# Hybrid decoder trunk on one core: block inverse by 32x32 and 64x64 products, scale sums on VectorE, key products by quarters, gates in row groups, accumulating DMAs

## The chip, the core and the metric

The kernel runs on one core of a Trainium2 chip. The metric is device time in microseconds, one launch, one core. PE is TensorE (matrix products into PSUM, weight loads beside them), DVE is VectorE, ACT is ScalarE, POOL is GpSimd, SP is the engine whose queue starts the DMAs.

## What is computed

One layer on a sequence of 1024 tokens of width 1024, all in float32. The parts that the change touches:

```python
mod = c_act @ w_mod[l] + b_mod[l]
sh1, sc1, g1, sh2, sc2, g2 = jnp.split(mod[:, None, :], N_MOD, axis=-1)
h = rms_norm(x, norm_mix_w[l]) * (1.0 + sc1) + sh1
proj = h @ w_in[l]
...
r_pre = jnp.einsum('bsgi,gij->bsgj', xb, lru_gate_a_w[l]) ...   # 8 blocks of 64x64
i_pre = jnp.einsum('bsgi,gij->bsgj', xb, lru_gate_x_w[l]) ...
...
decay = jnp.exp(jnp.where(causal, g[..., :, None] - g[..., None, :], -jnp.inf))
Lmat = jnp.where(strict, jnp.einsum('bhnid,bhnjd->bhnij', k_beta, k) * decay, 0.0)
tmat = Lmat + jnp.eye(C, dtype=jnp.float32)
u = lax.linalg.triangular_solve(tmat, v_beta, ...)
w = lax.linalg.triangular_solve(tmat, k_beta * jnp.exp(g)[..., None], ...)
...
mix = jnp.concatenate([out_lru, out_gdn], axis=-1) @ w_out[l]
x = x + g1 * mix
x = x + g2 * (jnp.square(jax.nn.relu(h @ w_up[l])) @ w_down[l])
```

## The kernel before

**Stages.** Tokens are normalised and transposed into `hT` (eight blocks of 128 channels, each as a rounded high part and a low remainder). Then 24 projections of 128 columns each run over all tokens: four keys k, four z, four pairs q and v, four pairs lx and ly. Keys feed the gated delta rule with chunks of 128 tokens (32 chunks: 4 heads by 8), lx and ly feed the RG-LRU. The output projection (`wg` for the delta rule's half, `wl` for the LRU's half), the second norm, and the MLP by a scheme of seven products (`upx`, `upy`, `upz`, then `dn`) follow and are not touched by the change, apart from their order.

**Precision.** The large products take three float32r products each (high by high, high by low, low by high: `mm3`, L575). Small ones are plain float32, which the trace shows as two PE instructions per product.

**Order.** Nothing is issued where it is written. `Recorder.add` (L220) records every operation; `schedule` (L267) simulates the engines with cost constants and writes one order per engine; `emit` plays it. Products marked `bb` (the large ones) give way to any small product that is ready. `SHIFTS`, a packed table, moves single operations by priority. So a change to any cost constant or to `SHIFTS` can reorder all queues.

**Start.** The SP queue loads x tiles 0 to 3, the eight tiles of the scale `sc1` (4 MB in runs of 512 columns), the key weights k0 and k1, `wab`, x tiles 4 to 7, then eight tiles for `sh1` (L676 to L691). `sc1` is a vector-matrix product done in two halves (L795 to L814): five of eight rows are summed on ACT and DVE (`macc`), three more and the sum are added by PE products with one output row (`sc_r`), copied to a row and turned into a column by PE (`sc_c`). Only when both halves are there are all `hT` blocks scaled, and the thirds of k0 and k1 (342 tokens each, `third`) can run. The key loop ends with k2 and k3 in line with the other projections (L1223).

**Weights.** `Proj.split` (L731) rounds a weight tile on ACT (`_wh`) and subtracts it on POOL or DVE (`_wl`).

**Decay and the block inverse.** `decay` (L912) loads the broadcast gate sums, adds the mask on POOL and takes eight ACT exponentials; it runs for each key and once more for each query. `key` (L933) multiplies the decay by `bcoef` (beta over the key's squared norm), multiplies it into k k^T and leaves the result in `LT`; `inverse` (L968) then

- solves the 32x32 diagonal blocks by 31 DVE steps of two instructions (`gg`, `xx`, `ftmp`),
- spreads them into 128x128 block-diagonal matrices `xn`, `xt`, with POOL clearing,
- and combines by four rounds of 32 products of 128x128 float32: `ie`, `ig`, `ih`, `ix`.

`chain` (L1097) then walks the eight chunks of a head with `LT`.

**LRU.** `lru` (L1182) convolves lx, splits the result on ACT and POOL (for the last block on DVE: `xrl`), and multiplies it by the gate weights, padded from two 64x64 blocks to 128x128 (`gwt`, `gwh`, `gwl`): for each of four channel blocks, two gates and two token halves three products of 512 tokens, 48 in all. `msum` gathers the squares on POOL.

Of the kernel before, what the change touches and what calls it, by code (L numbers as in the profile page):

```python
# [22 lines left out]
P = 128  # L23
# [24 lines left out]
SC1_SUM = 5  # L48
# [3 lines left out]
LOAD_WINDOW, DUE = 40.0, 5.0  # L52
RESERVE = {"b": 11, "ps": 2, "u": 1, "c": 2}


class Buf:


    def __init__(self, pool, tag, bufs, shape, dt, name, proto):
        self.pool, self.tag, self.bufs, self.shape, self.dt, self.name, self.proto = pool, tag, bufs, shape, dt, name, proto  # L60
        self.tile = None
        self.key = (id(pool), tag)
        self.left = 0
        self.last = 0.0
        self.held = False
        self.pri = 1e9
        self.sum = None
# [53 lines left out]
def dram_box(ap):  # L121
# [7 lines left out]
    'c-qaId2m(NeaC<AJ?ZI5LLdnV0RkZwiG4R<wm^)7YrMprIwncm)J@}Qn;B2s&a}-;-8P+MlCeAWA6YtW)=nmlGmY(z3C0fC21AT77@NiHn8ip4f%'  # L129
    'X-NC;j^Qo%_IG`(AS%vFr1jyS#hvx%Zsk`7Phy@0^#`w7v|jSNWjw&9C+Kw%f@gO~HjJheRg#*x5f{vi-x<OUf<RRC=f{IG#@j$BiBGF_eaG+uxu'  # L130
    '0_O5~3b>G0Eo_FtW8hH2o?GNZ}bLLu6`uV|I2Oq!m-usK({d=@J9o>#ro%nn2TN|U~Tjz`hBr-xS>2PV$J)AF+Cp1UWdXn=AvOzcNo4S+p<+4r>>'
    'JBZW=2VGGLP|vScKMQ|ptuytP<iOeyG!JI@<94#*(2j*TY9S``wv_^qcQ2=dxP4?`w|%*$N08LF27ZW(gu-Q$&nr{<=Z<{KGCHgZWuq-$QNZmUx5'
    'c>>3N9^anz>?dL=SODr7p8lqK>xxHO<m@}~UTd)}p2`uZeWySBrDv~H1IaQ?JTme0sy$<Mtd_p$h9_+xZJFKLHX@XadOEL-Gv@`ko(z0Tr`9eT-|'
    'cSor4XrfN5V>!~K)ux~NliYl%=KJkh<oeWsZ1n3{MzJ2cpc_*!Cvs%Cl*&jcW-Qmnb|)su&GhEH7Sr$JT1k&9C11u%4Zn@XaMq|J<Q<*HHk!@1rI'
    'qxwRR`$%zc&6%zI0(jU4DJlz}4eY%rke$47n94Kcq*IxM?z5=DE=+N5X_(CdKW%C8#q<or&xR>8b6FVw^Q;5{<2+$31YjO;78AETpnL_o#QR@!nt'
    'Q)^42{uZG8QYWHg#&CHcv#_S&Sdba$D%;H|I6lC<R2dj~$P9@S*A#;$?2iT8fw5s6Wbe^tdtmZIc(>b%+2{_uVWpWCB_Aqvpa#-hiw{s#gwNlE@`'
    'qgUDb)G!@Pd%r3GFzwWEBcRm99#CfdqV@VYvbFFlrN`mWyo$L<D7&?v(dEAprc8+P|B8%jKtWRv=zx*s9$@L{B68*DEt++el@v@!|4u3J=f47-Ks'
    'C>(>lt1B`8DC+NA8%X7r#6%A*~(@V$x93N-yLEX5l66fG-*!#i)#4i>Pj&TMPg9*|!k5#Qnb5p2>^Tz`V?VaDX!+?^w%XwfKISS|DE^DLPxeR|nS'
    'T~8Tw{Z6A>X?i#SHF8ZeT4nNM?;nX}DCM1bP?1M(hC9lpd<}XU64{Pjt&=v+_R3G>Tk<co=iBl_`0)s5tB`_G@1t>!mNP!99NmuePj)mP9<7zn%A'
    'K;1^F`2DSs?duoQn^gBa>u3GUQ*1y=(MlfdX#IQmS4;vOgX_o5xoFv3#rB`zwLO$E3@<rs=(JX;=RmlR;Sh;DJhxLmbXftXmw*lFvRLlu?ddk2!z'  # L140
# [67 lines left out]
class Recorder:  # L208
# [58 lines left out]
    def schedule(self):  # L267
# [36 lines left out]
        while done < len(ops):  # L304
# [34 lines left out]
            for b in op.allocs:  # L339
# [15 lines left out]
                elif f[0][0] > t + 1e-6:  # L355
                    wait = ("t", f[0][0])
# [1323 lines left out]
```

## Time and profile before

| | |
|---|---|
| median of 3 runs | 1164.93 us (1164.21 to 1165.41) |
| span of the profiled execution | 1162.6 us |
| busy: PE, DVE, ACT, POOL | 1137.1, 834.6, 616.5, 371.4 us |
| mean DMA rate | 197 GB/s |
| mean granted PE clock | 0.997 |

The span runs from the first to the last instruction of the one profiled execution; the runs' times also hold what lies around it, 2.3 us by the median. A group's busy time counts time in which at least one of its matrix products was in the pipe; to price one product the distance between the starts of neighbours is the better measure, and the prediction uses that.

### The profile page before, as it was taken

Reading aid. Unit: us, or ns where it says so; the run is one execution under the profiler, and the core shown is the slowest. Engines: PE = TensorE matmul, PEld = TensorE weight load, DVE = VectorE, ACT = ScalarE, POOL = GpSimd, SP = SyncE. Lnnn points to the kernel's source line nnn. Section 1 sums busy time; section 2 is a strip of 40 time slices with the busy share of each in tenths; the row PEclk is TensorE's granted clock in tenths of the full one; section 3 lists DMA queues with packets and bytes.
Section 4 is the critical chain, followed back from the end, with each engine's and each line's share of the span. In section 5 each row is a group of like instructions: output and inputs, shape, how many; then the busy total and the mean of one; then the engine's idle time right before and its main releaser. Section 6 shows DMA issues by size and latency. Waiting matters only on the chain.

```text
span 1162.6 us, 15986 instructions
## 1 busy us (share of the span) xinstructions
PE 1137.1 (98%) x5952; PEld 979.8 (84%) x5952; DVE 834.6 (72%) x1123; ACT 616.5 (53%) x988; POOL 371.4 (32%) x221
## 2 busy tenths in 40 slices
PE   6899999999999999999999999999999999999997
PEld 3799999999999998887888888887888888888885
DVE  5778786687986879778776776766885583865563
ACT  5547445445547866477655555556644533363441
POOL 1329512253424463300003231311450057723030
PEclk9999999999999999999999999999999999999999
DMA  9623432544454462422276887773999956864541
GB/s 338 223 86 110 134 121 75 180 121 159 152 185 145 135 230 107 145 84 80 65 267 237 274 281 247 252 244 136 364 403 388 369 175 247 308 226 168 199 163 72
DMA packets 127151, 229.52 MB, mean 197 GB/s; under 512 B 10657, under 2 KB 51806, under 8 KB 127074
## 3 DMA queue, kind: packets, MB, share of 16 engines
q1 hardware_dynamic: 127074, 228.51, 56.7%
q8 instruction: 46, 0.75, 0.3%
q14 instruction: 31, 0.25, 0.1%
HBM read 171.83 MB, written 56.65 MB: 197 GB/s over the span
## 4 chain that ended last, share of the span: by engine, by line
PE 91%; DMA 3%; DVE 3%; ACT 1%; issue 1%; SPq 1%; POOL 0%; POOLq 0%; ACTq 0%
PE dn L427 26%; PE upx L427 15%; PE upz L427 8%; PE wg L427 4%; PE upy L427 4%; PE wl L427 4%; PE z_p L427 4%; PE lx_p L427 4%; PE q_p L427 4%; PE ly_p L427 4%; PE v_p L427 3%; PE k_p L427 2%; PE ch L427 2%; SPq L427 1%; DMA sh_w<-in_w_mod_dram 1%
## 5 line engine op out<-in xcount | busy, mean ns | idle before, releaser
L427 PE MATMUL upx<-h2h,U 128*128 128x512 f32 x512 | 168.0, 394 | 0.0
L427 POOL TENSOR_TENSOR wd<-wd,wd 128x512 f32<-128x512 f32 x32 | 49.9, 1568 | 214.4 <-DMA wd<-in_w_down_dram 163.4
L427 PEld LDWEIGHTS upx<-h2h,U 128*128 128x128 f32 x512 | 96.0, 188 | 22.5
L427 PE MATMUL upx<-h2l,U 128*128 128x512 f32 x256 | 100.8, 394 | 0.0
L427 DVE TENSOR_TENSOR U<-wu,U 128x512 fp32r<-128x512 f32 x112 | 85.0, 774 | 18.1 <-ACT U L427 17.9
L427 ACT ACTIVATE act<-act 128x512 f32<-128x512 f32 x112 | 70.3, 632 | 44.9 <-DVE act L427 43.2
L427 PE MATMUL upz<-h2h,U 128*128 128x512 f32 x256 | 85.0, 394 | 0.0
L427 ACT CAST U<-wu 128x512 fp32r<-128x512 f32 x112 | 66.8, 617 | 27.8 <-DVE wu L427 10.0
L427 PEld LDWEIGHTS upx<-h2l,U 128*128 128x128 f32 x256 | 48.1, 188 | 11.5
L427 PEld LDWEIGHTS upz<-h2h,U 128*128 128x128 f32 x256 | 48.1, 188 | 11.4
L427 DVE TENSOR_TENSOR act<-upz,ek 128x512 f32<-128x512 f32 x32 | 22.1, 690 | 40.1 <-PE upz L427 25.9
L427 ACT COPY ek<-upx 128x512 f32<-128x512 f32 x48 | 28.0, 584 | 42.6 <-PE upx L427 42.4
L427 PE MATMUL upz<-h2l,U 128*128 128x512 f32 x128 | 50.4, 394 | 0.0
L427 POOL TENSOR_TENSOR R<-R,R_5o 128x1024 f32<-128x1024 f32 x8 | 20.0, 2520 | 74.4 <-DMA R<-in_w_down_dram 63.2
L427 PE MATMUL upy<-h2h,U 128*128 128x512 f32 x128 | 42.7, 394 | 0.0
L427 POOL TENSOR_TENSOR ssq<-ssq,mhalf 128x1 f32<-128x1 f32 x16 | 11.6, 725 | 84.8 <-DVE ssq L427 84.8
L427 DVE TENSOR_TENSOR wu<-wu,wu 128x512 f32<-128x512 f32 x48 | 36.1, 759 | 0.5 <-DMA wu<-in_w_up_dram 0.4
L427 ACT ACTIVATE vn<-ch,bcoef 128x128 f32<-128x128 f32 x32 | 11.8, 368 | 45.0 <-PE ch L427 44.9
L427 PE MATMUL k_p<-hh,k_wh 128*128 128x342 f32 x96 | 31.9, 332 | 1.0 <-ACT hh L427 1.0
L427 PE MATMUL k_p<-hl,k_wh 128*128 128x342 f32 x96 | 32.0, 333 | 0.8 <-DVE hl L427 0.8
L427 PE MATMUL k_p<-hh,k_wl 128*128 128x342 f32 x96 | 31.9, 332 | 0.0
L427 PE MATMUL ly_p<-hh,ly_wh 128*128 128x342 f32 x96 | 31.7, 330 | 0.0
(574 smaller groups left out, 3719.3 us busy)
## 6 DMA issues: line engine op xcount, KB each, us to landing
L<-aod SPq DMA_DIRECT2D x56, 512.0 KB, 6.5
R<-in_w_down_dram SPq DMA_DIRECT2D x40, 512.0 KB, 5.9
wu<-in_w_up_dram SPq DMA_DIRECT2D x32, 512.0 KB, 5.0
aod<-as SPq DMA_DIRECT2D x64, 256.0 KB, 3.3
wd<-in_w_down_dram SPq DMA_DIRECT2D x32, 512.0 KB, 6.5
aod<-act SPq DMA_DIRECT2D x48, 256.0 KB, 2.9
x<-in_x_dram SPq DMA_DIRECT2D x16, 512.0 KB, 4.6
sc_w<-in_w_mod_dram SPq DMA_DIRECT2D x16, 512.0 KB, 7.2
```

The source lines that it names most:

```text
L427: op.fn(*[res(v) for v in op.a], **{n: res(v) for n, v in op.k.items()})
```

## The change

The diff does the following.

- **Scale sums.** `sc1` comes in four quarters of 256 columns; all eight rows of a quarter are summed on ACT (one) and DVE (seven); PE only turns the sum into a column.
- **Keys by quarters.** The weights of all four keys come as four tiles of two channel blocks each (`wk0` to `wk3`). A class `Key` multiplies, for tokens 0 to 511, each pair of channel blocks as soon as its quarter of `sc1` is known, then tokens 512 to 767 (`second(0)`) and 768 to 1025 (`second(1)`). The first pair runs in two halves of 256 tokens. DMA order at the start is rewritten for this; 36 products of constants (`warm`) are recorded at a lowest priority `FILL`.
- **Weights.** `Proj.split` writes minus the high part with ACT and lets a DMA from the POOL queue add the raw weight to it. The same is done for the LRU's low part; `msum` and the decay mask are also added by such DMAs.
- **Decay** is made once per head, stored to DRAM and loaded again by the query. `bcoef` leaves it and goes to the small blocks of the inverse, the key's gate factor goes from a POOL product to a factor in `chain`.
- **Inverse.** Blocks of 32 are joined to 64 by five 32x32 products per chunk (`level1`), blocks of 64 to 128 by two 64x64 products per chunk (`level2`).
- **Gates.** The two 64x64 blocks stay apart: each product contracts over 64 rows and gives both gates, in pairs on the two halves of the rows.
- **Order.** Planner constants (SP issue, DMA lanes, start) and `SHIFTS` are new.

```diff
+FILL, WARM, AB_DUR, GATE_DUR, L1A_DUR, L1B_DUR, L2_DUR = 1e6, 36, 0.85, 0.89, 0.12, 0.2, 0.14
...
+class Adder(Proxy):
...
+            self.rec.add("POOL", fn, (), {"out": out, "in_": in_, "accum_op": ALU.add}, [out], [in_, out], ADD_ISSUE)
...
+    GD = Adder(rec, "POOL", nc.gpsimd)
...
+    load_x(0)
+    load_sc1(0)
...
+    load_x(1)
+    load_wk(0)
+    load_x(2, 3)
+    for q in range(1, 4):
+        load_sc1(q)
+        load_wk(q)
+    load_x(4, 5, 6, 7)
...
             A.copy(self.w[0], raw)
-            e.tensor_tensor(out=self.w[1], in0=raw, in1=self.w[0].bitcast(F32), op=ALU.subtract)
+            A.mul(self.w[1], self.w[0].bitcast(F32), -1.0)
+            GD.dma_start(out=self.w[1].bitcast(F32), in_=raw)
...
+    def scale1(q):
+        acc = big(f"sc1_acc{q}")[:, 0:256]
+        for k in range(NK):
+            macc(acc, sc1_w[q, k // 4][:, k % 4, :], k)
+        pc = ps(f"sc1_c{q}")
+        for j in range(2):
+            mm(pc[:, j:j + 1], acc[:, j * P:(j + 1) * P], ones[:, 0:1])
...
+    for q in range(1, 4):
+        scale1(q)
+        splitk(q, V if q == 1 else G)
+        for k in (2 * q, 2 * q + 1):
             xhalf(0, k)
+        for h in range(NH):
+            projs[h].first(q, 0, 512)
+    warm = ps("warm")
+    for i in range(WARM):
+        mm(warm[:, i % 4 * P:i % 4 * P + P], ident, triu)
+        rec.ops[-1].bias = FILL
...
+    def decay(h):
+        dm = big(f"k{h}_dm")
+        SP.dma_start(out=v3(dm), in_=neg[:, None, :].to_broadcast([P, 8, P]))
+        GD.dma_start(out=dm, in_=gdr[h:h + 1, :].to_broadcast([P, T]))
...
+        def level1(g):
+            gs = slice(16 * g, 16 * g + 16)
+            p = ps(f"it{g}")
+            for q in range(16):
+                i, c = 16 * g + q, slice(32 * q, 32 * q + 32)
+                mms(L1A_DUR, [(p[blk[b + 1], c], LT[blk[b], i, blk[b + 1]], xnc[blk[b], i, :], True, True) for b in (0, 2)], 0.25)
...
+                mms(L1B_DUR, [(p[blk[0], c], tt[blk[1], i, :], xtc[blk[1], i, :], True, True),
+                              (p[blk[2], c], tt[blk[3], i, :], xtc[blk[3], i, :], True, True),
+                              (p[blk[1], c], xtc[blk[1], i, :], tt[blk[1], i, :], True, True)], 0.25)
...
+        def level2(h):
...
+            for q in range(8):
+                mms(L2_DUR, [(p[up, 64 * q:64 * q + 64], LT[lo, 8 * h + q, up], w[lo, q, :], True, True)], 0.5)
+            A.mul(w[up], v3(p, 64)[up], -1.0)
...
+                mms(L2_DUR, [(p[lo, 64 * q:64 * q + 64], w[up, q, :], LT[up, 8 * h + q, up], True, True)], 0.5)
+            V.tensor_copy(LT[lo, hs, up], v3(p, 64)[lo])
...
-        (V if ct == 3 else G).tensor_tensor(out=xl_, in0=xr, in1=xh.bitcast(F32), op=ALU.subtract)
...
+        A.mul(xl_, xh.bitcast(F32), -1.0)
+        GD.dma_start(out=xl_.bitcast(F32), in_=xr)
+        cs = slice(ct * P, (ct + 1) * P)
+        for s in halves:
+            pair = [ps(f"gate{ct}{s.start}{e}") for e in range(2)]
+            mms(GATE_DUR, [(p, w[64 * e:64 * e + 64, cs], x_[64 * e:64 * e + 64, s], i == 0, i == 2)
+                           for i, (w, x_) in enumerate(((gwh, xh), (gwh, xl_), (gwl, xh))) for e, p in enumerate(pair)])
+            for e, p in enumerate(pair):
+                r = slice(64 * e, 64 * e + 64)
+                A.activation(ta[r, s], p[0:64, :], AF.Tanh, scale=0.5, bias=hab[r, ct:ct + 1])
+                A.activation(ti[r, s], p[64:128, :], AF.Tanh, scale=0.5, bias=hxb[r, ct:ct + 1])
```

396 lines of the change are left out of this document (224 added, 172 removed).

## The prediction

> **What bounds the kernel now.** First the page, then busy time by stretches, then PE's waits.
>
> ```profile
> span 1162.6 us, 15986 instructions
> PE 1137.1 (98%) x5952; PEld 979.8 (84%) x5952; DVE 834.6 (72%) x1123; ACT 616.5 (53%) x988; POOL 371.4 (32%) x221
> ```
> ```profile
> 0.00:15.00 15.00, 7.29 (x29) 4.57 (x30) 7.01 (x20) 7.96 (x12) 4.26 (x13) 1.00 0.86 316
> 15.00:30.00 15.00, 12.57 (x54) 5.87 (x52) 9.30 (x25) 9.50 (x16) 1.65 (x3) 1.00 1.07 363
> 30.00:45.00 15.00, 11.46 (x66) 9.17 (x66) 11.41 (x15) 9.35 (x14) 0.55 (x1) 0.93 0.79 286
> 45.00:60.00 15.00, 14.49 (x95) 12.90 (x94) 11.04 (x23) 5.08 (x8) 8.02 (x3) 0.96 0.54 146
> 60.00:1140.00 1080.00, 1076.36 (x5649) 935.41 (x5650) 788.02 (x1028) 578.91 (x928) 354.68 (x197) 1.00 0.56 195
> ```
> ```profile
> PE h2T L427 <- DVE h2r L427: 1.1, 2, 0.6
> PE ktok L427 <- DVE k2T L427: 0.9, 1, 0.9
> ```
>
> The columns of the second fence are the stretch and its length, then busy time of PE, PEld, DVE, ACT and POOL, the granted clock, the DMA share and GB/s. From 60 to 1140 us PE is idle 3.6 us of 1080; its longest wait is 1.1 us in total. So from 60 us on PE products are the bound: a microsecond of PE work removed there is a microsecond of the end, and work moved off POOL is worth nothing by itself. Up to 60 us PE is idle 14.2 us, and at times slowed (clock 0.93 and 0.96). To price PE work I use distances between starts, from the chain of waits, where products stand back to back:
>
> ```profile
> 119.58 33.12 PE z_p L427 x211
> ```
> ```profile
> 843.31 306.12 PE dn L427 x1320
> ```
>
> A three-part product of 342 columns costs 33.12 / 211 = 0.157 us per part, of 512 columns 306.12 / 1320 = 0.232.
>
> **The start.** Here PE's time up to 60 us is divided into work that any version must do and the rest.
>
> ```profile
> L427 PE MATMUL xTp<-ident,x 128*128 128x128 f32 x64 | 12.7, 332 | 1.7 <-ACT x L427 0.8 <-DVE rs L427 0.3 <-DVE x L427 0.2
> L427 PE MATMUL k_p<-hh,k_wh 128*128 128x342 f32 x32 | 11.2, 352 | 1.0 <-ACT hh L427 1.0
> ```
> ```profile
> L427 PE MATMUL k_p<-hh,k_wl 128*128 128x342 f32 x31 | 10.8, 349 | 0.0
> L427 PE MATMUL sc_r<-sc_w,cact 128*1 128x512 f32 x12 | 5.8, 591 | 1.4 <-DMA sc_w<-in_w_mod_dram 1.3
> L427 PE MATMUL ab<-hl,wab 128*16 128x342 f32 x16 | 5.1, 323 | 0.0
> ```
> ```profile
> L427 PE MATMUL sc_c<-ones,sc_row 1*128 1x1 f32 x16 | 2.1, 248 | 0.0
> L427 PE MATMUL sc_r<-sc_acc,ones 128*1 128x512 f32 x4 | 2.0, 592 | 0.0
> L427 PE MATMUL sh_c<-ones,sh_acc 128*128 128x1 f32 x15 | 1.7, 245 | 0.0
> ```
>
> Lasting work: 95 parts of k at 0.157 (14.9; 32, 32 and 31 in three groups), 32 of ab (5.0; two groups of 16), 64 transposes at 0.112 (7.2; that distance is shown below), sh_c 1.7: 29 us. The other 31 us of the 60 are loss: idle, slow clock, 9.9 us of `sc_r` and `sc_c`, pipe ends. How much of it is lost after the change follows from what comes when:
>
> ```profile
> GB/s 0 38 385 391 388 385 404 396 385 392 384 389 381 307 273 234 426 410 421 407 385 410 421 401 410 315 39 6 189 288 149 249 238 120 29 285 46 0 172 178
> ```
> ```profile
> 11.55 3.11 DVE L427 SCALAR_TENSOR_TENSOR sc_acc<-sc_w,cact,sc_acc 128x512 f32<-128x512 f32 x4 [0.70 <-ACT sc_acc L427]
> ```
> ```profile
> 22.01 2.73 DVE L427 SCALAR_TENSOR_TENSOR hl<-xTp,A,hh 128x512 fp32r<-128x512 f32 x4 [0.74 <-ACT hh L427]
> ```
> ```profile
> 34.51 2.60 DVE L427 SCALAR_TENSOR_TENSOR sh_acc<-sh_w,cact,sh_acc 128x1024 f32<-128x1024 f32 x2 [0.89 <-ACT sh_acc L427]
> ```
> ```profile
> 145.79 0.43 DVE L427 TENSOR_TENSOR ftmp<-gg,xx 128x256 f32<-128x256 f32 x1
> ```
>
> The first row has the DMA rate from 0 to 60 us in 40 slices: about 388 GB/s from 2 us on, so a tile of 0.524 MB takes 1.35 us. In the new order x0 and the first scale quarter (three tiles) are there at 1.5 + 4.1 = 5.6 us. DVE then adds seven rows of 256 columns (0.43 each by the last row, as a row of 512 costs 3.11 / 4 = 0.78), 3.0 us, with one scaling of x between (at most the 1.3 of a row of 1024 columns, 2.60 / 2): 9.9 us; column product, two short DVE steps and the first eighth of `hT` end at about 13 us, as I estimate,, where the key products begin. From there PE has 24 parts per quarter at 0.232, for four quarters 22.3 us (twice as many at half the price where 256 columns are taken), and 32 transposes, 3.6: until 38.9 us. Behind it the DMA needs 1.5 + 16 x 1.35 = 23.1 us for all sixteen tiles, DVE 12.0 for scale sums (28 x 0.43 instead of 8 x 0.78 = 6.2), 5.8 for `hl` (six of 2.73 / 4 = 0.68 and four of 0.43), at most 7.8 for six steps of 1024 columns on x and the weights, 25.6 us in all, starting at 6: both ahead of PE. Next come x4 to x7 (28.5 us), and `second(0)` with the two first thirds of ab, 96 at 0.116 and 32 at 0.157, 16.1 us of PE. That covers the sums for `sh1` (tiles at 39 us, seven DVE rows of 1.3 us, 9.1 us), on which only `second(1)` waits; were they late, PE would be idle by that much. Loss then: 13 us before the first product, `sc_c` 1.8 (16 instructions of 1.7 / 15, like sh_c), and 4 us that I put for seams between these four sequences: 19 instead of 31, **gain 12**. Ends: 16 (no seams), and -2, if the 5.8 us more DVE work stands in the way and the 36 `warm` products (72 instructions at 0.112, 8.1 us) stand in PE's queue ahead of ready work instead of in gaps.
>
> **The inverse.** Before: the four groups `ie`, `ig`, `ih`, `ix`, 32 products and 64 instructions each.
>
> ```profile
> 167.70 0.40 PE L427 MATMUL v_p<-hh,v_wl 128*128 128x342 f32 x1
> 167.94 0.32 PE L427 MATMUL v_p<-hh,v_wh 128*128 128x342 f32 x1
> ```
> ```profile
> 169.76 5.30 PE L427 MATMUL ie<-xn,LT 128*128 128x128 f32 x46
> 174.90 4.41 PE L427 MATMUL ig<-xt,ee 128*128 128x128 f32 x38
> ```
> ```profile
> L427 PEld LDWEIGHTS upy<-h2h,U 128*128 128x128 f32 x128 | 24.0, 188 | 5.6
> ```
> ```profile
> L427 PEld LDWEIGHTS ab<-hl,wab 128*16 128x16 f32 x24 | 2.3, 95 | 1.5 <-DVE hl L427 0.2
> ```
>
> From 169.76 to 174.90 stand 46 instructions: 0.112 each, so 256 cost **28.6 us**. After: 160 products of 32x32 and 64 of 64x64, 320 and 128 instructions. No row has both few weights and few columns. A weight load of 16 columns takes 95 ns, of 128 columns 188: 0.83 ns per column, so loads shrink with the block. If the whole distance shrinks so, with 5 ns fixed, it is 0.033 for 32 and 0.059 for 64: 10.6 + 7.6 = 18.2, with 16 changes of shape at 0.08 (1.3; the first of two parts of v after `ie` takes 0.24 to the next start and not 0.157) 19.5: **gain 9.1**. I take this one, as it is nearest to the load row and to 342 against 512 columns (0.157 / 0.232 against 0.67). Ends: 15.6, if the 32x32 products of a pair run side by side, and -22, if each instruction costs as much as sh_c's with one column, 1.7 / 15 = 0.113: 448 x 0.113 = 50.6. The DVE steps of the diagonal blocks stay; PE fills with z, q and v, as now.
>
> The Trainium skill, TensorE: Matmul & The Clock Gate, section "Wait — 56ns, not 53.3ns?", names two floors for the distance of small products, about 25 ns and, with another decoding, about 62 ns. By the first my 18.2 stands, by the second 448 instructions take 27.8 us; no run here shows which. Its page TensorEngine Tiling (Array Packing), "Gotcha 1: PSUM Pressure", says that row tiles can't use one PSUM bank at the same time, and `level1` writes its pair into one bank; that speaks against the end of 15.6.
>
> **Gates.** Three groups of 16 as this one, 48 x 0.232 = 11.1 us:
>
> ```profile
> L427 PE MATMUL gate<-xrh,gwh 128*128 128x512 f32 x16 | 5.4, 412 | 0.5 <-ACT xrh L427 0.5
> ```
>
> After: 48 of half the rows. In pairs they cost 24 x 0.232 = 5.6 and eight times two such seams, 6.9; one after the other 11.1 and the seams. No row shows two products at once. I take a **gain of 4**, as the halves share neither rows nor bank; ends -1 and 5.
>
> **Accumulating DMAs.** A weight's low part was one POOL step; it becomes an ACT step and a DMA.
>
> ```profile
> 153.18 1.04 ACT L427 CAST v_wh<-v_w 128x1024 fp32r<-128x1024 f32 x1
> ```
> ```profile
> 154.29 2.39 POOL L427 TENSOR_TENSOR v_wl<-v_w,v_wh 128x1024 fp32r<-128x1024 f32 x1 [8.81 <-ACT v_wh L427]
> ```
> ```profile
> 163.79 0.32 PE L427 MATMUL v_p<-hh,v_wh 128*128 128x342 f32 x1
> ```
> ```profile
> z_w<-in_w_in_dram SPq DMA_DIRECT2D x3, 512.0 KB, 5.0
> ```
>
> No row has such a DMA. The lower end is the plain load, 5.0 us; the upper, of loads in a crowded queue, 10.8 (shown below). I take 5.5: this stage's queue is not crowded, but the transfer has two inputs. Ready is then 1.04 + 5.5 - 2.39 = 4.2 us later, and v_wl was ready 7.1 us before PE used it: covered, price 0. If it is not, every one of the 20 later projections waits, and on POOL's queue the next steps stand behind. The ACT steps (20 x 1.04, and 16 more gate evictions) are off the path at 53% ACT. One place has little cover, the last LRU block, whose low part DVE made:
>
> ```profile
> 439.73 1.21 DVE L427 TENSOR_TENSOR xrl<-xr,xrh 128x1024 fp32r<-128x1024 f32 x1
> ```
> ```profile
> 473.98 1.30 POOL L427 TENSOR_TENSOR lcl<-lcm,lch 128x512 fp32r<-128x512 f32 x1
> ```
> ```profile
> 477.07 0.19 PEld L427 LDWEIGHTS wl<-wo0h,lch 128*128 128x128 f32 x1
> ```
>
> That block goes on through gates, scan, DRAM and `lcl`, ready 1.8 us before `wl`. It becomes later by 1.04 + 5.5 - 1.21 = 5.3, so `wl` waits 3.5 us: **loss 3.5**. Ends 0 (DVE and POOL are freed ahead of it) and 9. Decay, key factor and `msum` leave POOL; PE never waited for them: 0, ends -3.6 (the idle time above) and 4.
>
> **Sum.** 1162.6 - 12 - 9.1 - 4 + 3.5 = 1141.0 us of span. The runs' median lies 2.3 us over that span, so 1143 us.
>
> **Rivals.**
> 1. *Small instructions have a floor* of some half of the 0.112: 448 x 0.0625 = 28.0, gain 0.6 and not 9.1, **1152**. For it: no row below 0.1 exists; against: loads shrink. The skill's second floor would be this case.
> 2. *The start stays bound by DVE*: its sums and splits, with `warm` in the way, eat the 12 us: **1155**. For it: DVE is busy 11.4 of 15 us at 30 to 45 us; against: it waits for DMA and ACT before that.
> 3. *Slower: accumulating DMAs come late.* The place is each of the 20 projections from z0 to ly3. The slack of 7.1 us is used up when a DMA lands later than 8.5 us, and each further microsecond costs 20; from 9.6 us the kernel is slower than before. At the crowded landing time of this row it is 20 x 2.3 = 46, **1189**.
>
> ```profile
> sc_w<-in_w_mod_dram SPq DMA_DIRECT2D x8, 512.0 KB, 10.8
> ```
> Against it: in this row eight tiles wait for one another, later in the kernel they don't.
>
> 4. *More is won*: no seams at the start (4), 32x32 pairs side by side (5.3): **1134**.
> 5. *Small products cost as much as full ones*: inverse 50.6 and not 19.5, 31 us over the forecast, **1174**.
>
> **Chances.** Forecast 0.46 (own range 1136 to 1150), rival 1 0.17, rival 2 0.14, rival 3 0.09, rival 4 0.11, rival 5 0.03. A measurement here tells 0.2%, 2.3 us, from no change. Slower: rivals 3 and 5 and a little of mishaps in the new order, 0.13; same 0.03; faster 0.84. The range goes from 1126 (rival 4 and the gates' upper end) to 1166 (rival 2 with rival 1); rivals 3 and 5 are left out.
>
> **What would show it.** PE's first key product at about 13 us and less than 6 us idle from there to 60 us (step 1); distances of 0.033 and 0.06 us in the inverse (step 2); two gate products starting almost together (step 3); DMAs on POOL's queue landing within 6 us, and no PE wait on a `_wl` tile (step 4); a wait of some 3 us at the first `wl` (step 5). Wrong it would be if PE idles over 10 us between 60 and 1140 us, as the sum rests on PE staying the bound.

## The result, and the profile after

| | before | after |
|---|---|---|
| median of the runs, us | 1165.12 (1164.21 to 1166.99) | 1163.45 (1161.52 to 1166.83) |
| ratio to before, 95% interval | | 0.9989 (0.9979 to 1.0000) |
| span of the profiled execution, us | 1162.6 | 1162.9 |

Of the 22 us that the prediction promised, 1.7 are there, which is not told from no change. The page of the changed kernel shows that TensorE did less work and ended no sooner:

```profile
span 1162.9 us, 16590 instructions
...
PE 1129.3 (97%) x6224; PEld 974.9 (84%) x6224; DVE 800.4 (69%) x1136; ACT 635.3 (55%) x982; POOL 268.9 (23%) x188
```

PE is busy 7.8 us less (1137.1 before). The same stretches as in the prediction tell more (stretch, length, busy time of PE, PEld, DVE, ACT, POOL, granted clock, DMA share, GB/s):

```profile
0.00:15.00 15.00, 2.49 (x9) 1.78 (x9) 8.22 (x26) 5.72 (x10) 2.25 (x10) 1.00 0.85 299
15.00:30.00 15.00, 13.41 (x82) 12.64 (x83) 14.30 (x31) 11.12 (x19) 3.69 (x3) 1.00 1.07 374
30.00:45.00 15.00, 15.00 (x79) 12.47 (x77) 8.47 (x19) 10.28 (x16) 5.35 (x5) 1.00 0.96 350
45.00:60.00 15.00, 15.00 (x120) 14.35 (x119) 13.43 (x27) 10.84 (x19) 1.89 (x2) 1.00 0.66 166
60.00:1140.00 1080.00, 1061.53 (x5810) 914.56 (x5810) 748.30 (x1024) 592.27 (x910) 253.86 (x166) 0.98 0.65 213
```

From 60 us on PE now idles 18.5 us (3.6 before), and the clock, 1.00 before, is 0.98. PE's waits there, in total, how often, and the longest:

```profile
PE lrus L414 <- DMA msum<-lsq: 4.3, 1, 4.3
PE iy L592 <- issue: 4.2, 2, 3.0
PE iw L592 <- DVE aw L414: 3.9, 1, 3.9
PE gate L592 <- DMA xrl<-xr: 3.4, 1, 3.4
PE h2T L414 <- DVE h2r L414: 2.0, 4, 0.5
PE h2T L414 <- ACT h2r L414: 0.7, 1, 0.7
```

Where the lead went is read from the first start of the same product in both kernels. Rows of the view by tile (count; shortest, median and longest in ns; first to last start), before and then after:

```profile
L427 PE MATMUL q_p<-hh,q_wh x96: 312/319/404, 152.5 to 284.9; 128*128 128x342 f32 x96
L427 PE MATMUL lx_p<-hh,lx_wh x96: 313/319/405, 305.4 to 413.5; 128*128 128x342 f32 x96
L427 PE MATMUL upx<-h2h,U x512: 387/394/482, 527.8 to 840.1; 128*128 128x512 f32 x171
```
```profile
L414 PE MATMUL q_p<-hh,q_wh x96: 313/320/423, 140.4 to 277.7; 128*128 128x342 f32 x96
L414 PE MATMUL lx_p<-hh,lx_wh x96: 313/319/487, 295.0 to 404.3; 128*128 128x342 f32 x96
L414 PE MATMUL upx<-h2h,U x512: 387/394/422, 527.0 to 839.2; 128*128 128x512 f32 x171
```

The lead is 12.1 us when the q projections start, 10.4 at lx, 0.8 at the MLP. So two distances describe every kernel below: from the first `q_p` to the first `lx_p` (the inverse lies in it; 152.9 before, 154.6 after) and from there to the first `upx` (gates and `wl`; 222.4 before, 232.0 after).

**The inverse.** Four stretches of the changed kernel; all four of before have PE at 10.00 and the clock at 1.00:

```profile
190.00:200.00 10.00, 5.82 (x322) 5.15 (x321) 9.78 (x12) 6.61 (x11) 0.00 (x0) 0.86 0.51 162
200.00:210.00 10.00, 6.14 (x48) 5.78 (x48) 9.21 (x9) 3.79 (x6) 1.35 (x1) 0.50 0.35 107
210.00:220.00 10.00, 10.00 (x87) 9.54 (x86) 3.98 (x6) 5.24 (x8) 2.36 (x2) 0.50 0.69 181
220.00:230.00 10.00, 10.00 (x80) 9.07 (x80) 6.80 (x15) 2.37 (x6) 2.38 (x1) 0.95 0.49 157
```

Idle are 4.18 + 3.86 = 8.0 us. Busy time at a lower clock loses 5.82 x 0.14 + 6.14 x 0.50 + 10 x 0.50 + 10 x 0.05 = 9.4 us (8.9 by stretches of 1 us, as most of the first row's busy time ran at full clock). From the timeline of PE (start, duration, instructions, idle time before and what ended it), and of VectorE:

```profile
190.09 2.15 PE L592 MATMUL it<-xnc,LT 32*32 32x32 f32 x124
...
193.02 0.21 PE L592 MATMUL iy<-xtc,ttc 32*32 32x32 f32 x2
193.04 0.19 PE L592 MATMUL iy<-ttc,xtc 32*32 32x32 f32 x1
193.05 0.21 PE L592 MATMUL iy<-xtc,ttc 32*32 32x32 f32 x2
...
199.42 0.21 PE L592 MATMUL iy<-ttc,xtc 32*32 32x32 f32 x1 [3.01 <-issue]
...
205.72 5.53 PE L592 MATMUL iw<-aw,LT 64*64 64x64 f32 x48 [3.86 <-DVE aw L414]
```
```profile
197.35 3.92 DVE L414 SCALAR_TENSOR_TENSOR g_acc<-g_w,cact,g_acc 128x1024 f32<-128x1024 f32 x3
201.18 1.28 DVE L414 SCALAR_TENSOR_TENSOR v1T<-v_st,cols,v1T 128x1024 f32<-128x1024 f32 x1
...
204.89 1.28 DVE L414 SCALAR_TENSOR_TENSOR aw<-iy,bcoef 32x512 f32<-32x512 f32 x2
```

The products themselves are cheap: an instruction of `it` takes 2.15 / 124 = 0.017 us, three of `iy` take some 0.03 (193.02 to 193.05). In the trace the two instructions of a pair of `it` start 0.007 us apart, and the next pair follows 0.025 us later. But between the levels stand evictions, and `aw<-iy` is late because VectorE has 7.5 us of other work queued ahead of it.

**The start of `wl`.** Three stretches of the changed kernel:

```profile
465.00:470.00 5.00, 0.69 (x7) 0.68 (x7) 4.60 (x2) 0.97 (x2) 2.90 (x2) 1.00 1.05 291
470.00:475.00 5.00, 5.00 (x19) 4.42 (x19) 3.21 (x5) 2.78 (x6) 2.57 (x2) 0.52 0.78 254
475.00:480.00 5.00, 5.00 (x19) 3.95 (x19) 2.64 (x5) 0.27 (x1) 0.73 (x1) 0.80 0.00 0
```

4.3 us idle, the wait of `lrus` for `msum`, and then 5 x 0.48 + 5 x 0.20 = 3.4 us of clock. With the waits of `h2T` (2.7 us, 1.1 before) the stage loses 9.3 us.

### The profile page after: what moved, and what is told of

The parts are those of the page before. It is cut to its first block, busy times and chain, and to the rows that moved or that the text cites. A ratio compares the mean times of both kernels' runs of the same rounds, so it can differ in the third digit from the quotient of the medians.

```text
span 1162.9 us, 16590 instructions
## 1 busy us (share of the span) xinstructions
PE 1129.3 (97%) x6224; PEld 974.9 (84%) x6224; DVE 800.4 (69%) x1136; ACT 635.3 (55%) x982; POOL 268.9 (23%) x188
## 4 chain that ended last, share of the span: by engine, by line
PE 86%; DVE 5%; ACT 4%; DMA 3%; issue 2%; POOL 0%; SPq 0%; POOLq 0%; DVEq 0%; ACTq 0%
PE dn L414 27%; PE upx L414 15%; PE upz L414 8%; PE k_p L414 4%; PE z_p L414 4%; PE q_p L414 4%; PE upy L414 4%; PE wl L414 4%; PE v_p L414 3%; PE lx_p L414 2%; PE ch L414 2%; PE ly_p L414 2%; DVE xr L414 1%; PE cho L414 1%; DMA sc_w<-in_w_mod_dram 1%
## 5 line engine op out<-in xcount | busy, mean ns | idle before, releaser
L414 POOL TENSOR_TENSOR wd<-wd,wd 128x512 f32<-128x512 f32 x32 | 45.6, 1427 | 233.1 <-DMA wd<-in_w_down_dram 187.8
L414 DVE TENSOR_TENSOR U<-wu,U 128x512 fp32r<-128x512 f32 x112 | 78.1, 714 | 15.9 <-ACT U L414 15.8
L414 PE MATMUL k_p<-hh,wkh 128*128 128x256 f32 (+2 forms) x104 | 30.9, 327 | 1.4 <-ACT hh L414 1.4
L414 PE MATMUL lx_p<-hl,lx_wh 128*128 128x342 f32 x96 | 32.1, 334 | 0.0
L414 PE MATMUL lx_p<-hh,lx_wl 128*128 128x342 f32 x96 | 32.0, 333 | 0.0
L414 PE MATMUL lx_p<-hh,lx_wh 128*128 128x342 f32 x96 | 31.7, 330 | 0.0
L414 PE MATMUL q_p<-hh,q_wl 128*128 128x342 f32 x96 | 31.5, 328 | 0.0
```

What stands on the lines that cost most here:

```text
L414: op.fn(*[res(v) for v in op.a], **{n: res(v) for n, v in op.k.items()})
```

## The experiments

All are edits of the changed kernel. To keep the order of everything else, most edit the list that `schedule` returns, just before it is played; the numbers are places in the recorded program, `move(what, after)` puts operations behind another. Sums are moved from a DMA to GpSimd in place: `GD.add` records the same entry for the planner and issues a tensor_tensor.

```diff
+    def add(self, out, in_):
+        self.dma_start(out=out, in_=in_)
+        op = self.rec.ops[-1]
+        op.fn, op.k = self.nce.tensor_tensor, {"out": out, "in0": out, "in1": in_, "op": ALU.add}
```

Each ratio is to the kernel before on the same chip, with its 95% interval; the distances come from each kernel's profiled execution, and first starts of `q_p` scatter by 2.2 us among them (139.6 to 141.8). Kernels whose inverse has the same order differ by up to 1.4 us on the first distance (154.2 to 155.6), after, no_warm and aw_first by 0.9 us on the second. The medians come from different chips; where the intervals of two ratios overlap, the runs do not tell the two kernels apart. That holds between the changed kernel and no_warm, msum_pool, xrl_pool, aw_first, lru_pool, lru_order and inv_batch: for these the distances are the evidence.

| kernel | median, us | ratio to before (95%) | `q_p` to `lx_p`, us | `lx_p` to `upx`, us |
|---|---|---|---|---|
| after | 1163.45 | 0.9989 (0.9979 to 1.0000) | 154.6 | 232.0 |
| no_warm | 1163.32 | 0.9989 (0.9981 to 0.9998) | 154.5 | 231.6 |
| msum_pool | 1165.29 | 1.0005 (0.9996 to 1.0014) | 154.2 | 231.4 |
| xrl_pool | 1162.91 | 0.9987 (0.9978 to 0.9996) | 154.2 | 229.0 |
| aw_first | 1165.38 | 1.0004 (0.9995 to 1.0013) | 155.0 | 232.5 |
| lru_pool | 1163.39 | 0.9981 (0.9972 to 0.9989) | 155.6 | 230.0 |
| lru_unscaled | 1159.42 | 0.9943 (0.9930 to 0.9957) | 154.8 | 225.7 |
| inv_order | 1161.60 | 0.9962 (0.9949 to 0.9974) | 152.6 | 230.8 |
| all_three | 1161.67 | 0.9961 (0.9949 to 0.9974) | 152.7 | 230.7 |
| inv_mixed | 1172.67 | 1.0070 (1.0056 to 1.0085) | 161.7 | 230.9 |
| lru_order | 1162.73 | 0.9982 (0.9972 to 0.9991) | 154.6 | 227.9 |
| both | 1169.20 | 1.0036 (1.0024 to 1.0048) | 162.4 | 230.0 |
| inv_batch | 1163.32 | 0.9985 (0.9975 to 0.9995) | 151.5 | 233.2 |
| batch_lru | 1159.32 | 0.9943 (0.9931 to 0.9955) | 151.1 | 231.1 |
| wl_order | 1160.74 | 0.9965 (0.9952 to 0.9977) | 154.8 | 226.8 |
| best | 1155.21 | 0.9919 (0.9905 to 0.9932) | 152.4 | 226.0 |

### The tail: no_warm

```diff
+        order = [i for i in order if self.ops[i].bias != FILL]
```

> The 72 instructions of `warm` are left out (nothing reads them); everything else stands in the same order. In the changed kernel's trace they run from 1153.8 to 1161.8 us, behind the last product of `dn`. Theory A, they set the end: the span falls from 1162.9 by up to 5 us. Theory B, the output's own chain (VectorE, then its DMA) ends no earlier than they do: less than 1 us. Both expect every time before 1150 us unchanged.

The profiled span fell from 1162.9 to 1161.3 us, 0.5 of it already at `upx`: the fillers hold the end by some 1.1 us. The median can't tell it. They were put at the lowest priority and run behind everything, so they fill no gap.

### One wait at a time: msum_pool, xrl_pool, aw_first

```diff
-            GD.dma_start(out=msum, in_=sq)
+            GD.add(out=msum, in_=sq)
```

> The three sums into `msum` are made by GpSimd's tensor_tensor instead of an accumulating DMA; the order written out is the same. Theory A, the DMA alone makes the stall ahead of `lrus` (4.3 us of idle time, and 3.4 us of half clock after it): 6 to 8 us faster. Theory B, the next thing is as late: `wo1h` ends at 470.1 us and `wo1l` at 471.3 us in the trace, where `lrus` starts at 469.4, so TensorE waits there instead: 0 to 2 us faster, with the wait at `wl` put down to ACT or DVE `wo1`. GpSimd's own add (2.4 to 3.4 us before) also pushes `wo2l` and `wo0l` back.

Theory B in kind: `lrus` started at 464.4 us instead of 469.4, and PE then stood in front of the next factor, `wo0l` and not the `wo1` that was named. No time was won.

```profile
PE wl L414 <- POOL wo0l L414: 4.1, 1, 4.1
```

```diff
-        GD.dma_start(out=xl_.bitcast(F32), in_=xr)
+        GD.add(out=xl_, in_=xr)
```

> The four differences `xrl` are finished by GpSimd's tensor_tensor instead of an accumulating DMA; the order written out is the same. Theory A, the DMA makes the 3.4 us of idle time at the second block's gates and the low clock after it (0.73 at 370 to 380 us): 3 to 6 us ahead at `wg`, and so at the end. Theory C, the lead is lost again at `wl`: under 2 us at the end, with a longer wait there.

Theory A holds for the stall: no idle time and full clock at the gates, the last `ly_p` product at 412.4 us instead of 418.0. Theory C holds for the end: of these 5.6 us 2.3 are left at `upx`, 0.5 in the median, and PE waits longer ahead of `wl`. The waits of that kernel that were not there before:

```profile
PE wg L414 <- DVE x L414: 3.8, 1, 3.8
...
PE lrus L414 <- DVE wo L414: 2.0, 1, 2.0
```

```diff
+        late = [1541, 1543, 1545, 2076, 1547, 2077]   # g1_acc, v1T
+        order = [i for i in order if i not in late]
+        n = order.index(1135) + 1                     # the second aw<-iy
+        order[n:n] = late
```

> Six VectorE instructions (four of `g1_acc`, two of `v1T`) are put behind the two evictions `aw<-iy`, which they preceded; all else is as it was. Theory A, the inverse loses its time to VectorE's queue, and the idle time is what lets the clock fall: `iw` starts near 200 us instead of 205.7, the clock stays over 0.9, and the kernel is 8 to 14 us faster. Theory B, the small products themselves let the clock fall: `iw` starts near 200 us and the clock still stands at 0.50 for some 15 us; 4 to 6 us ahead at `ch`. Theory C, what is won here is lost again at `wl`, where VectorE and ScalarE end last: under 2 us at the end whatever is won at 200 us.

`iw` started at 201.3 us, as both A and B had it, but the clock stayed down, and then a product of the next level waited in ScalarE's queue, where the cast of `g1_acc` stood ahead of `aw<-iw`:

```profile
PE iz L597 <- ACT aw L419: 3.8, 1, 3.8
```
```profile
200.00:210.00 10.00, 8.89 (x69) 8.14 (x67) 9.90 (x10) 1.19 (x2) 0.00 (x0) 0.50 0.35 107
```

PE is busy 89% of this stretch and the clock is 0.50. So A's second half (idle time alone lets the clock fall) doesn't hold; C isn't decided, as nothing was won that could be lost.

### Several at once: lru_pool, lru_unscaled, inv_order, all_three

lru_pool has both `GD.add` lines. lru_unscaled also leaves out the instructions that scale `wo0` to `wo3`, so the rows of W_out go into `wl` unscaled and the output is no longer the layer's:

```diff
+        scale = [i for i, o in enumerate(self.ops) if o.eng == "DVE" and o.fn.__name__ == "scalar_tensor_tensor"
+                 and {b.name for b in o.bufs} & {"wo0", "wo1", "wo2", "wo3"}]
+        order = [i for i in order if i not in scale]
```

> Both sums at once on GpSimd, `xrl` and `msum`, in the same order. Alone, the first brought TensorE 5.6 us ahead at the end of `ly_p` and 2.3 us at `upx`, the second nothing (the wait went to `wo0l`). If the DMAs were the cause, the two together give some 9 us. If VectorE and GpSimd hand over the last factors of `wl` no sooner (theory C), `upx` starts 2 to 4 us before the changed kernel's 527.0, and TensorE waits 3 us or more at `wg` and `wl` for VectorE or GpSimd.

> As lru_pool, and the four VectorE instructions that scale `wo0` to `wo3` ahead of `wl` (2.3 to 6.4 us each in the trace) are left out, so that the rows of W_out are used unscaled. Theory C (VectorE's queue and the port that it shares with GpSimd set the start of `wl`): the waits at `wg`, `lrus` and `wl` all but vanish and it is another 3 to 6 us faster than lru_pool. Theory A (the DMAs alone): within 1 us of lru_pool.

lru_pool gains 2.0 us on the second distance and not 9; four VectorE instructions less gain another 4.3 (225.7 against 230.0), and 4.0 in the median. So the start of `wl` is set in good part by what VectorE and GpSimd hand over: the DMAs were the wait that came last, not the only one. After both edits the second distance is still 3.3 us over the 222.4 of before.

```diff
+        move([1086, 1083], 1097)
+        move([2076, 2077, 1541, 1543, 1545, 1547], 1135)
+        move([1551, 1552], 1164)
+        move(list(range(2181, 2200)), 1134)
```

> The inverse's stage alone is put in another order: the two stray products of `iy0` go with the others; the three products of `v1T` and four of `g1_acc` go behind `aw<-iy` on VectorE; the cast of `g1_acc` goes behind three `aw<-iw` on ScalarE; the 19 products left of `q2_p2` go behind `iy` on TensorE. Theory A (queues of VectorE and ScalarE): no wait of TensorE over 1 us between 190 and 225 us, `ch` starts near 213 instead of 223.2, 7 to 10 us ahead at `lx_p`. Theory B (the small products let the clock fall): the clock is 0.50 for 10 us or more though TensorE never idles, and 4 to 7 us ahead at `lx_p`. Theory of the fetch: the 1.2 and 3.0 us of unexplained idle time at `iy` stay, now ahead of `q2_p2`. Theory C: at the end under 2 us of it is left.

2.0 us ahead on the first distance, less than expected: the wait moved once more, to `vtok`, for `v1T` (4.6 us). The clock fell too, to 0.50 at 198 to 202 and 214 to 220 us. Of what was won, some was kept: `upx` started at 523.0 instead of 527.0 (0.7 us of that was there at the first `q_p`), 1.8 us in the median and 3.1 by the ratios, so C, with its mark of 2 us, is neither shown nor ruled out. And at full clock `iw` ran at 3.01 / 48 = 0.063 us per instruction:

```profile
205.04 3.01 PE L602 MATMUL iw<-aw,LT 64*64 64x64 f32 x48
```

The 1.2 and 3.0 us of unexplained idle time were still there, inside `iy` as before.

all_three joins inv_order with both `GD.add` lines of lru_pool and leaves out the fillers, as no_warm does.

> inv_order and lru_pool together, without `warm`. Waits that only hand the time on (theory C): the gains don't add up, and the end comes 2 to 5 us sooner than in the changed kernel, with the longest wait of TensorE at `wg` or `wl`. If each lost time had its own cause: the sum of the two, 10 us or more.

The two distances are those of inv_order (152.7 and 230.7): the gain of lru_pool was not added. PE waited for `wo0l` (4.4 us) and `gcl` (2.2).

### Mixing, and the order at `wl`: inv_mixed, lru_order, both

inv_mixed puts the 19 products one or two at a time between the groups of `iy1`:

```diff
...
+        iy, rest = [1130, *range(1119, 1130), *range(1131, 1135)], list(range(2181, 2200))
+        for n, i in enumerate(iy):
+            move(rest[n * 19 // 16:(n + 1) * 19 // 16], i)
+        move([2076, 2077, 2078, 1541, 1543], 1135)
...
+        move([1545, 1547, 1549, 1551, 1552], 1173)
...
```

> As inv_order, with the 19 products of `q2_p2` placed between the small products of `iy1` instead of behind them, all of `v1T` ahead of `g1_acc` on VectorE, three products of `g1_acc`, its casts and its row products behind the inverse. Theory of the fetch (TensorE used up its instructions faster than they came): with 3 us of other work among the small products the unexplained idle time falls from 4.2 us to under 2.5 us. Theory that these gaps are a wait that the trace hides: they stay at 4 us, at the same products. No wait for `v1T` (4.6 us in inv_order): `ch` starts at 214 to 217 us, where it started at 221.9; 6 to 9 us ahead of the changed kernel at `lx_p` (inv_order: 2.8). At the end 5 to 8 us faster than the changed kernel if TensorE's lead carries through `wl`, 2 to 4 us if it doesn't.

A miss, and the most telling one. 7.1 us slower on the first distance, 9 in the median. The unexplained gaps shrank (4.2 to 1.1 us), but:

```profile
200.00:210.00 10.00, 10.00 (x78) 6.19 (x78) 0.00 (x0) 1.27 (x3) 0.00 (x0) 0.50 0.10 30
```
```profile
196.25 0.65 PE L428 MATMUL q_p<-hh,q_wh 128*128 128x342 f32 x1
197.09 0.65 PE L428 MATMUL q_p<-hl,q_wh 128*128 128x342 f32 x1
```

One full product and one group of three small ones (six instructions) took 0.84 us, at a clock of 0.50, with PE never idle. So in this run a mixture of mostly small products went with a low clock for 16 us, and each change between the two seems to cost. Not all of the 7.1 us is that: the last products of `iz` waited 5.1 us for ScalarE's `aw`, because here, as in aw_first, the cast of `g1_acc` stood ahead of it.

```diff
-            GD.dma_start(out=msum, in_=sq)
+            (GD.add if ct == 3 else GD.dma_start)(out=msum, in_=sq)
...
-        GD.dma_start(out=xl_.bitcast(F32), in_=xr)
+        (GD.add(out=xl_, in_=xr) if ct == 1 else GD.dma_start(out=xl_.bitcast(F32), in_=xr))
...
+        move([3854, 3862], 3861)   # wo0l, wo2l behind wo2h
```

> Only the accumulating DMAs that TensorE waited for are made GpSimd sums (`xrl1` and the last of `msum`), and GpSimd's `wo0l` and `wo2l` are put ahead of that sum, so that nothing of `wl` stands behind it. Theory C (what comes last at `wl` is VectorE's and GpSimd's queue): no wait over 1.5 us at `gate`, `lrus` and `wl`, `upx` starts 5 to 8 us before 527.0, and the kernel is as much faster. If the lead is lost there whatever is done: under 3 us.

4.1 us on the second distance, 0.7 in the median: `lrus` still waited 2.3 us for GpSimd's sum, the third block's gates 2.2 for their DMA.

both joins inv_mixed with lru_order, without the fillers.

> inv_mixed and lru_order together, without `warm`. If what is lost in the inverse and what is lost at `wl` are separate: the sum of the two gains, 10 to 15 us faster than the changed kernel, some 1150 us. If what is won ahead of `wl` is lost at `wl`: no faster than the better of the two.

No faster than the better of the two; the loss of inv_mixed at the inverse (162.4) went through to the end. A loss there isn't absorbed at `wl`.

### Batches: inv_batch, batch_lru

```diff
+        for fill, i in (((2181, 2186), 2180), ((2186, 2194), 1083), ((2194, 2200), 1134), ((2203, 2215), 1950), ((2215, 2227), 1179)):
+            move(list(range(*fill)), i)   # behind it, iy0, iy1, qk, iw
...
+        move([1545, 1547, 1549, 1551, 1552], 1191)
...
```

> The inverse's stage in batches: behind `it`, each half of `iy`, the `qk` products and `iw` stand 2 to 12 full projection products (19 of `q2_p2`, 24 of `q2_p0`, moved up whole, not one by one); evictions of the inverse stand ahead of `g1_acc` on VectorE and ScalarE. In the changed kernel 8.0 us of idle time and 9.2 us of low clock are lost between 180 and 240 us. Theory B' (a long stretch of small products alone lets the clock fall; full products every 2 to 3 us keep it up): the clock stays over 0.9, the two losses fall from 17.2 to under 7 us, `lx_p` starts 8 us or more before 295.0, and the kernel is some 8 us faster. Theory B (any small products keep it at 0.50): the clock is 0.50 for 10 us or more all the same, and under 4 us are won. Theory of the mixture (each change between small and full products costs 0.2 us or more, as in inv_mixed): here there are some ten changes, so it costs 2 us at most.

The clock followed B', the idle time did not (8.3 us between 180 and 240 us, 8.0 in the changed kernel):

```profile
190.00:200.00 10.00, 7.84 (x320) 7.06 (x313) 6.74 (x9) 5.47 (x10) 0.00 (x0) 1.00 0.67 208
200.00:210.00 10.00, 10.00 (x105) 9.29 (x104) 8.22 (x8) 7.70 (x11) 0.00 (x0) 1.00 0.20 60
210.00:220.00 10.00, 6.59 (x87) 6.06 (x85) 9.20 (x11) 1.23 (x3) 0.86 (x1) 0.93 0.86 245
```

It stayed at 1.00 through `it`, `iy` and `iw`, and the last `iz` started at 215.1 us instead of 222.4. Of these 7 us 5.2 were then given up again: this edit had put `g1_acc` and its cast ahead of the recurrence's first `vn` on ScalarE.

```profile
PE ch L427 <- ACT vn L427: 5.2, 1, 5.2
```

So the first distance fell by 3.1 us only, and the second rose by 1.2. The median is the changed kernel's.

batch_lru joins inv_batch with lru_order, without the fillers.

> inv_batch and lru_order together, without `warm`. lru_order alone brought `upx` 3.6 us forward in its trace. If the two add up and the batches keep the clock: 10 to 12 us faster than the changed kernel, some 1152 us. If the lead of inv_batch is lost at `wl`: no faster than lru_order, 1162 us.

4.1 us faster than the changed kernel in the median, between the two cases. The second distance shows why it isn't more: 231.1, where lru_order has 227.9. Between 455 and 490 us both idle 4.2 us, but the low clock costs 4.5 us here and 1.7 there (by stretches of 1 us); why it fell more is open. Both also pay for GpSimd's new order, as VectorE's steps are drawn out while GpSimd works. The same scan in the changed kernel and in batch_lru (4.49 us in lru_order too), with GpSimd's steps beside it:

```profile
456.88 2.28 DVE L414 TENSOR_TENSOR_SCAN xr<-aa,xr 128x1024 f32<-128x1024 f32 x1
```
```profile
450.53 4.49 DVE L429 TENSOR_TENSOR_SCAN xr<-aa,xr 128x1024 f32<-128x1024 f32 x1
...
449.49 3.38 POOL L429 TENSOR_TENSOR wo0l<-wo,wo0h 128x1024 fp32r<-128x1024 f32 x1
452.84 4.39 POOL L429 TENSOR_TENSOR wo2l<-wo,wo2h 128x1024 fp32r<-128x1024 f32 x1
```

### Both places mended: wl_order, best

```diff
+        first = [3867, 3880, 3922, 3935]   # four groups of wl
+        move([i + k for i in first for k in (0, 1, 2, 6, 7, 8)][1:] + [3569, 3570, 3571, 3572, 3568, 3574, 3575, 3573], 3867)
+        move([i + k for i in first for k in (3, 5, 4, 9, 10, 11)], 3850)
```

> lru_order, and the first four groups of `wl` begin with the rows of W_out that are there early: 24 products with `wo0` and `wo2`, then `lrus`, then their 24 products with `wo1` and `wo3`. What came last in lru_order and batch_lru were the sum on GpSimd (`lrus` waited 2.3 us), `wo1l` and `lcl`, and the clock after it (0.50 to 0.52 for 10 us). If these are all: idle time and low clock between 455 and 490 us fall from 5.8 us in lru_order to under 1.5 us, and `upx` starts 3 to 5 us before lru_order's 523.4. If the last LRU block is later still: the wait goes to `lch` or `lcl` of its rows (`lcm3`) and 1 us or less is won.

The second case: the wait went to `lcl` (2.4 us), the low part of the rows of the last LRU block; 1.1 us on the second distance.

best joins this with batch_lru and leaves `g1_acc` in VectorE's idle time ahead of `aw` (`move([2076, 2077, 2078, 1547, 1549], 1135)`, `move([1551, 1552], 2289)`).

> batch_lru with wl_order's products, and with `g1_acc` where neither the inverse nor the first `vn` of the recurrence waits for it (5.2 us in inv_batch). If nothing else comes in their place: idle time and low clock between 180 and 240 us fall from 9.8 to under 4 us, those between 455 and 490 from 8.6 to under 1.5, and it is 10 to 13 us faster than the changed kernel, 1150 to 1153 us. If the lead is lost at `wl` again: 1158 us or more.

1155.2 us, 8.2 less than the changed kernel and 9.3 (0.81%) less than before on the same chip, the best of all. By the table's distances 2.2 us come from the inverse and 6.0 from the way to the MLP. It missed the 10 to 13 us, and both marks: between 180 and 240 us idle time and low clock take 11.8 us (6.7 and 5.1), between 455 and 490 us 5.6. `ch` waited 4.9 us and `wl` 3.0 for `lcl`. In the longest wait of `ch`, 4.1 us, VectorE itself stood idle with no releaser in the profile, so what held it is open. And the clock fell in the inverse, though PE has the same order of products from 187 to 210 us as in inv_batch and batch_lru:

```profile
190.00:200.00 10.00, 8.79 (x335) 7.80 (x333) 9.81 (x11) 5.75 (x8) 0.00 (x0) 0.87 0.61 182
200.00:210.00 10.00, 10.00 (x94) 9.49 (x88) 9.49 (x10) 5.61 (x10) 0.00 (x0) 0.79 0.29 90
```

batch_lru has 1.00 in both stretches. So the batches are not enough to be sure of the clock.

## Why the prediction was wrong

The span missed the forecast by 21.9 us (1162.9 against 1141.0): 10.8 in the inverse's stretch (9.1 to be won, 1.7 lost), 10.1 from the gates to the MLP (0.5 to be won, 9.6 lost) and 1.1 for the fillers at the end. The time does lie in the range of 1126 to 1166 us, but near the end that stood for rivals 2 and 1 together; neither came true, so this is chance. (The terms named for the two ends come to 1133 and 1163.5, not to 1126 and 1166.)

**The start, right.** Forecast 12 us, 12.1 measured when the q projections begin; ahead of that point both kernels have the same products but for the start's own. With the scatter of first starts it is 10.7 to 12.9. Two parts of the working were off and partly cancel: the first key product came at 17.5 us and not at 13, and from 15 to 60 us PE idled 1.6 us where 4 us of seams were put. `warm` did not stand in the way, since it ran at the very end.

**The inverse, wrong; here half of the forecast failed.** The prices were not the fault: 0.017 us for a 32x32 instruction against 0.033, 0.063 for 64x64 against 0.059. Rivals 1 and 5 (a floor, or the full price) fell with them, and the 15.6 us of the best case were there as work: `it` 128 x 0.017 = 2.2, `iy` 64 x 0.03 = 1.9, `iw` and `iz` 128 x 0.063 = 8.1, together 12.2 instead of 28.6. The step that failed is the half sentence "PE fills with z, q and v, as now". Before, it was not z, q and v that filled: after the `ie` at 169.76 us that the prediction shows, the next product of a projection starts at 196.91.

```profile
196.91 0.40 PE L427 MATMUL v_p<-hh,v_wh 128*128 128x342 f32 x1
```

The inverse filled its own gaps, as 32 products of 128x128 in a round cover the evictions of the round before. Now a level takes 1 to 4 us, its evictions stand behind 7.5 us of other VectorE work, and hardly any other products stand between the levels. 8.0 us of idle time and some 9 us of clock ate the 16.4 us won. inv_batch shows that the order is at fault: with full products between the levels and the evictions ahead, the clock stood at 1.00 until the last `iz`, and that started 7.3 us sooner. inv_order, which moved the projection products behind `iy` in one piece, had it only 1.3 us sooner. Why the clock falls is open (see the end).

The prediction used the rule of the Trainium skill, TensorEngine Tiling (Array Packing), "Gotcha 1: PSUM Pressure", against the pair in one bank. The trace differs: the two instructions of a pair of `it` start 0.007 us apart and write into one bank, at 0.017 us per instruction on average. So a pair does run side by side, and 0.032 us is the price of the pair.

**Gates, right in mechanism.** A pair starts together (two instructions every 0.23 us), so their work fell by 5.5 us, a little over the upper end of 5. But they stood behind the DMA of `xrl`: 3.4 us idle, and a clock of 0.73 at 370 to 380 us and 0.93 after it cost 2.5 (6.62 x 0.27 + 10 x 0.07):

```profile
370.00:380.00 10.00, 6.62 (x33) 5.14 (x32) 8.07 (x6) 7.66 (x11) 0.86 (x1) 0.73 1.05 239
380.00:390.00 10.00, 10.00 (x61) 10.00 (x60) 3.31 (x4) 8.28 (x12) 0.00 (x0) 0.93 0.15 54
```

**Accumulating DMAs.** For the projections the price of 0 held: they landed in 4.9 to 8.1 us (medians by tile) and no `_wl` tile was waited for, so rival 3 fell. The loss of 3.5 us at `wl` was mis-sized and misplaced. The wait was not for `xrl` of the last block but for `msum`, of which the prediction said, with the decay and the key factor, "leave POOL; PE never waited for them: 0". That held only while GpSimd's sum was early; as a DMA it took 6.3 us (median), and with the clock behind it 7.7 us went, beyond the 4 that had been allowed. And msum_pool and lru_unscaled show that it hid VectorE's and GpSimd's queue, which would have taken most of it anyway (without the DMA's wait nothing was won, without VectorE's four steps 4.3 us more): PE came 10 us early and met a chain (scan, squares, `wo` factors) that was only 2 us early. The last squares, from ScalarE's timeline, before and after:

```profile
462.87 1.07 ACT L427 ACTIVATE lsq<-ly_st 128x1024 f32<-128x1024 f32 x1
```
```profile
460.97 1.06 ACT L414 ACTIVATE lsq<-ly_st 128x1024 f32<-128x1024 f32 x1 [2.85 <-DVE ly_st L414]
```

**The sign of failure was named.** "PE idles over 10 us between 60 and 1140 us": it idled 18.5. What the sum lacked is a check, for each gain ahead of that point, of whether the other engines come as much sooner.

## What to carry to other kernels

When products get small, price the evictions between them and what is queued ahead of those, not only the products; put full products between the levels in batches, not one by one (the clock stayed up so in two traces of three). A gain of PE far ahead counts as far as the next hand-over of another engine, so look up, at each such place, how early the others are. A wait that a profile names is the last of several: each time one was taken away here, the next came up.

## What the runs showed of the hardware

- **The clock stays low under small products though PE is busy.** 0.50 at 10.00 of 10 us busy (the changed kernel from 210 to 220 us, mostly 64x64 products; inv_mixed from 200 to 210 us) and 0.50 at 8.89 (aw_first). The Trainium skill, TensorE: Matmul & The Clock Gate, "What's actually happening", sets the gate by how busy PE has been; by these rows busy time isn't the measure, the kind of products counts too. With the same products in batches of 1 to 4 us between full ones the clock stayed at 1.00 until the inverse was done in inv_batch and batch_lru, but in best, in the same order, it stood at 0.50 from 198 to 204 us, with PE busy all the time. Over all runs the mean clock is 0.981 to 0.987 for the changed kernel, 0.985 to 0.994 for inv_batch, 0.990 to 0.992 for batch_lru and 0.992 to 0.994 for best. So batches go with a higher clock. What makes it fall is open, and the gaps inside `iy` (next point but one) are a rival: the first was 0.7 and 0.6 us long in inv_batch and batch_lru and 1.1 to 1.7 us in the other fourteen traces, in all of which the clock fell, during it or up to 3 us behind it.
- **Changing between tile sizes seems to cost.** In inv_mixed one 342-column product and three 32x32 ones (six instructions) took 0.84 us at a clock of 0.50. Back to back at full clock they take 0.157 and some 0.06, at half clock then 0.44: the 0.40 us left over I put down to the two changes. The changed kernel has it once at full clock: from the `v_p` product at 187.57 us over four instructions of `it` to the second `v_p` after them, at 188.27, pass 0.69 us, where 2 x 0.157 + 4 x 0.017 = 0.38 would do; 0.31 are left. No run measured the changes by themselves.
- **A run of tiny products seems to outrun the supply of instructions.** Two gaps with no releaser, 1.2 us to 194.87 and 3.0 to 199.42 us, stand 128 products apart, with their weight loads 256 instructions. In the traces of the changed kernel and of all fifteen edits the first gap stands after 1366 PE products, and the second, where there is one, 128 products later, whichever products the order had put there. So the gaps belong to a place in PE's stream of instructions, not to a tile or an eviction. The DMA view of 192 to 193 us and that of 197 to 198 us each have one packet of the instruction queue (count, MB, share), elsewhere one in 10 to 20 us:

```profile
q8 instruction: 1, 0.02, 6.1%
```

  With 19 full products among them the gaps shrank to 1.1 us (inv_mixed), with batches to 2.2. That PE waits there for a fetch is read from these packets; no run varied the fetch alone, so it is supported, not shown.
- **VectorE and GpSimd slow each other.** The scan of 2.28 us took 4.49 beside GpSimd's tensor_tensor. It ended at 455.02 us, 2.15 us after GpSimd's first step (452.87), and GpSimd's second step, begun at 452.84, ended 2.21 us after the scan: as if each had waited for the other to finish. This agrees with the Trainium skill, SBUF — State Buffer, "SBUF: two separate sides", which has the two engines share a port pair under an exclusive lock.
